# Expert weights of a mixture of experts: one plain unit of twelve in place of two, the token gate moved into the product of gate and up, a later release of the outcome buffers, and the weights of a further block requested together

## The chip, the cores and the metric

The kernel is one program on one NeuronCore of a Trainium2 chip, in one launch. The metric is the device time of that program in microseconds (us); less is better.

## The reference

Two blocks run one after the other over a sequence of 1024 tokens of width 1024, everything in float32. The first block is two layers of gated recurrences (they are not touched by the change). The second block is two layers, each an attention mixer, a layer norm with a scaled residual, and a mixture of experts of which each token uses two of 32:

```python
def hierarchical_moe(h, w_group, b_group, w_expert, b_expert, w_gate, w_up, w_down):
    ...
    gates = g_prob * e_prob
    experts = g_idx * EXPERTS_PER_GROUP + e_local
    ...
    def expert_block(args):
        xb, e = args
        return (jax.nn.silu(xb @ w_gate[e]) * (xb @ w_up[e])) @ w_down[e]

    ys = lax.map(expert_block, (xs, block_expert)).reshape(n_rows, D)
    ys = ys * row_gate[:, None].astype(ys.dtype)
    out = jnp.zeros((N + 1, D), ys.dtype).at[row_tok].add(ys)[:N]
    return out.reshape(B, S, D)
```

`xb` is 128 tokens by 1024, `w_gate` and `w_up` are 1024 by 512 per expert, `w_down` is 512 by 1024.

## The kernel before, in words

**What the expert stage does.** Per layer it walks over 32 experts of 128 places each. For one expert GpSimd (POOL) clears a buffer and gathers the expert's tokens into it (an indirect DMA, `slot<-xb`). TensorE (PE) transposes them: 8 transposes of 128x128 (`banks<-c,slot`, c being the unit matrix). ScalarE (ACT) and VectorE (DVE) turn the result into two rounded parts, high and low (`split`). Matmuls with gate and up follow, SiLU on ACT, the product `a` on DVE, 4 transposes of `a`, its split, and the matmuls with down. DVE multiplies the outcome by the token's gate and by a vector of the layer (`gn`) into a buffer `y`, and POOL scatters `y` with addition into the array Y in HBM (an indirect DMA, `Y<-slot`). The last expert keeps its outcome on the chip.

**Units.** The weights of one expert are 12 units of 128x1024 (512 KB): 4 of gate, 4 of up, 4 of down. A unit is used in one of two ways. A **split** unit is first rounded by ACT to a high part (`slot<-slot 128x1024` on ACT), then DVE subtracts to get the low part (`slot<-slot 128x1024` on DVE), and PE runs three products of these for each half, 6 matmuls of 512 columns. A **plain** unit is multiplied as it is, in full float32, against an unsplit copy of the transposed tokens (`xf`, in the tile named small): 2 matmuls in the program, 4 rows `banks<-slot,small` in the trace. `PLAIN` (L2479) names the plain units: unit 0 (the first of gate) and unit 4 (the first of up).

**What sets the order.** The program is written by cooperating chains of Python generators (`Flow`, L115). Each engine has a modelled clock, and the chain whose modelled time and priority come first records its next instructions; so the order on each engine follows from a model, and every engine then runs its list strictly in that order. Buffers are slots of 128x1024 in an arena (`Arena`, L281): `take` hands out the free slot with the smallest free time, and `give` notes as free time the modelled end of the last work on the slot (12 us after the issue for a scatter with addition). A slot that is taken again while its last work still runs on the chip makes the next writer wait.

**Chains of the stage.** `Experts.load` requests units in order on the queue of SyncE (SP), with at most `limit` units requested and not yet used up; `limit` is set to 20 while the output projection before the stage frees its slots (L1630), and to 22 when the stage starts (L2850). `Experts.split` splits at most `SPLIT = 6` units ahead of the one that PE has used last. `moe_experts` keeps up to two experts open, so that the transposes and the gate matmuls of the next expert stand among the down matmuls of the one before.

**The further block.** An expert with more than 128 tokens needs more blocks. `moe_extra` (L2712) holds a loop with a trip count that is known on the chip only, ahead of the 32 experts; its body is one `expert` whose weights come from `Direct` (L2693): 4 requests for gate at its first use, then for up and down, each at its own first use and behind the gather (`K.fetched`). In this input layer 0 makes no trip and layer 1 makes one.

**Rows ahead of the stage.** `Rows.put` (L1471) writes a finished tile of tokens: a modulated copy for the gather (`also`) and, after an affine step on POOL, the residual into Y.

All instructions of engines bear line L72 in the profile (a wrapper records them) and all DMAs of SP line L185.

## Time and profile before

| what | value |
|---|---|
| median of 3 runs | 4220.27 us |
| lowest and highest of them | 4214.49 and 4231.77 us |
| profiled execution, its own time | 4222.61 us |
| its span, first to last instruction | 4220.1 us |
| mean granted TensorE clock of the span | 0.957 |
| busy share of PE, DVE, ACT, POOL | 92%, 74%, 50%, 22% |
| expert stage of layer 0 in the trace | about 2035 to 2672 us |
| expert stage of layer 1 (with the further block) | about 3486 to 4170 us |

The profiled execution took 4222.61 us and its span is 4220.1 us, so 2.5 us lie around the span; it is 2.3 us above the median. Rows of the timeline give the start, the busy time, the engine, and in square brackets the idle time before the instruction with what ended it. The mean over the program hides the stages: with two expert stages of some 640 us each, rows by stretch tell more than the shares above.

### The profile page before, as it was taken

To read this page: it belongs to the slowest core of one execution; us is meant where nothing else is said; L and a number is where in the kernel's file an instruction comes from. 1 tells how busy PE (TensorE), PEld (TensorE's weight loads), DVE (VectorE), ACT (ScalarE), POOL (GpSimd) and SP (SyncE) were. 2 spreads that over 40 slices of the span, in tenths; PEclk is the share of its full clock that TensorE was granted. 3 is DMA by queue.
4 is the path that set the end of the run, shared out by engine and by line. 5 is a ranking of instruction groups with operands and counts; after the bars stand their busy time and mean duration, and the time that the engine had idled before them with its cause. 6 is when DMAs were issued, how large, how long until landed. Compare 5 with 4: busy or idle time off the path is not lost. (4 is left out here: it accounts for less than half of the span.)

```text
span 4220.1 us, 62468 instructions
## 1 busy us (share of the span) xinstructions
PE 3896.1 (92%) x22870; PEld 3126.8 (74%) x22870; DVE 3119.8 (74%) x5891; ACT 2118.6 (50%) x3866; POOL 946.2 (22%) x638
## 2 busy tenths in 40 slices
PE   7999999999999999969799999889999967999996
PEld 6888788788887777857577777677777765777774
DVE  7777766775767788686777777666667686777776
ACT  4333335342333555431466666667779415666663
POOL 2111100221113223354322222310001351222222
PEclk9999999999999999979899999999999978999998
DMA  4232322111113444234799998300011246999993
GB/s 150 80 98 84 95 90 92 42 42 51 53 61 120 146 131 135 68 122 153 269 356 357 355 355 314 117 11 21 16 53 41 96 161 226 353 351 357 360 353 128
DMA packets 338763, 682.11 MB, mean 162 GB/s; under 512 B 59957, under 2 KB 190703, under 8 KB 338453
## 3 DMA queue, kind: packets, MB, share of 16 engines
q1 hardware_dynamic: 320020, 644.95, 43.5%
q0 software_dynamic: 18432, 33.15, 3.2%
q8 instruction: 180, 2.95, 0.3%
q14 instruction: 131, 1.07, 0.1%
HBM read 625.89 MB, written 86.08 MB: 169 GB/s over the span
## 5 line engine op out<-in xcount | busy, mean ns | idle before, releaser
L72 PE MATMUL banks<-slot 128*128 128x512 f32 (+7 forms) x17868 | 3182.9, 344 | 78.7 <-DVE slot L72 44.1
L72 PEld LDWEIGHTS banks<-slot 128*128 128x128 f32 (+4 forms) x17868 | 2492.3, 178 | 643.6 <-issue 107.5
L72 DVE TENSOR_TENSOR slot<-slot 128x1024 fp32r<-128x1024 f32 (+14 forms) x1352 | 1308.2, 995 | 365.1 <-ACT slot L72 288.2
L72 ACT ACTIVATE slot<-slot 128x1024 fp32r<-128x1024 f32 (+5 forms) x946 | 927.0, 1009 | 876.6 <-PE banks L72 400.1
L72 ACT ACTIVATE slot<-banks 128x512 f32<-128x512 f32 (+8 forms) x1124 | 537.7, 497 | 677.0 <-PE banks L72 606.3
L72 POOL TENSOR_TENSOR slot<-slot 128x384 f32<-128x384 f32 (+3 forms) x270 | 452.7, 1696 | 1374.4 <-PE banks L72 402.0
L72 PE MATMUL banks<-c,slot 128*128 128x128 f32 (+2 forms) x3484 | 519.0, 285 | 118.3 <-DVE slot L72 53.9
L72 PEld LDWEIGHTS banks<-c,slot 128*128 128x128 f32 (+1 forms) x3484 | 430.8, 159 | 235.2 <-issue 66.6
L72 ACT ACTIVATE slot<-slot,small 128x1024 f32<-128x1024 f32 (+1 forms) x292 | 265.8, 924 | 197.3 <-DVE small L72 193.6
L72 PE MATMUL banks<-slot,small 128*128 128x512 f32 (+2 forms) x648 | 294.0, 573 | 49.1 <-ACT small L72 39.2
L72 DVE TENSOR_TENSOR slot<-banks,slot 64x512 fp32r<-64x512 f32 (+6 forms) x492 | 257.0, 551 | 62.5 <-ACT slot L72 52.5
L72 DVE COPY slot<-banks 128x512 f32<-128x512 f32 (+6 forms) x406 | 220.1, 551 | 103.7 <-PE banks L72 79.6
L72 POOL MEMSET slot<- 128x1024 f32 (+1 forms) x70 | 66.6, 957 | 940.3 <-PE banks L72 750.7
L72 PEld LDWEIGHTS banks<-slot,small 128*128 128x128 f32 x648 | 116.4, 213 | 105.3 <-ACT small L72 50.8
L72 POOL DMA_INDIRECT Y<-slot,small x62 | 144.0, 2322 | 198.5 <-DVE slot L72 183.5
L72 DVE TENSOR_REDUCE small<-banks 128x1 f32<-128x1024 f32 x128 | 154.4, 1220 | 45.7 <-PE banks L72 44.0
L72 ACT ACTIVATE slot<-banks,small 128x1024 f32<-128x1024 f32 x140 | 156.5, 1121 | 61.3 <-DVE small L72 60.5
L72 DVE TENSOR_TENSOR slot<-slot,banks 128x512 f32<-128x512 f32 (+3 forms) x175 | 116.5, 670 | 88.3 <-PE banks L72 88.0
L72 DVE SCALAR_TENSOR_TENSOR slot<-slot,c_act 128x1024 f32<-128x1024 f32 x84 | 121.0, 1442 | 29.4 <-DMA slot<-in_ada_w 22.7
L72 DVE SCALAR_TENSOR_TENSOR small<-small 128x1 f32<-128x1 f32 (+3 forms) x590 | 125.8, 220 | 12.6
L72 PE MATMUL banks<-small,slot 128*128 128x128 f32 (+1 forms) x576 | 105.4, 298 | 22.2 <-DVE small L72 18.4
L72 DVE SCALAR_TENSOR_TENSOR slot<-banks,cw,slot 128x511 f32<-128x511 f32 (+1 forms) x144 | 106.9, 746 | 6.0 <-ACT slot L72 3.9
(130 smaller groups left out, 1787.0 us busy)
## 6 DMA issues: line engine op xcount, KB each, us to landing
slot<-in_moe_w_up SPq DMA_DIRECT2D x260, 512.0 KB
slot<-in_moe_w_down SPq DMA_DIRECT2D x260, 512.0 KB
slot<-in_moe_w_gate SPq DMA_DIRECT2D x260, 512.0 KB
slot<-in_ada_w SPq DMA_DIRECT2D x96, 512.0 KB
slot<-in_w_in SPq DMA_DIRECT2D x56, 512.0 KB
xb<-slot SPq DMA_DIRECT2D x40, 512.0 KB
slot<-xb SPq DMA_DIRECT2D x24, 512.0 KB
slot<-in_na_w_qkv SPq DMA_DIRECT2D x24, 512.0 KB
```

The lines of the kernel that those rows point to most:

```text
L72: r = real(*a, **k)
```

## The change

It has six parts:

1. `PLAIN` becomes `(0,)`. Unit 4 is split like the others: 6 matmuls in place of 2 plain ones, one more rounding on ACT, one more subtraction on DVE, and the first half of the transposed tokens is split whole, not in its second 256 columns only.
2. The token gate moves: `a` becomes (SiLU times gate) times up in one DVE instruction, and `y` is a product of two.
3. `y` goes back to the arena when the scatter's modelled end has passed on the recording clock (`stored`), not at once; in the further block it goes back at once as before.
4. `Direct` requests all 12 units at the start of the loop's body, and splits the gate units right after the gather's issue (`first`).
5. The `limit` ahead of the stage is 16, not 20.
6. For the last two tiles of tokens `Rows.put` records the affine step and the write of Y only after the routing (`mid.late`).

```diff
+        if self.late is not None and t >= NT - 2:
+            yield self.late
         with K.F.aside():
             if self.early:
                 self.affine(K, x)
...
-        freed.limit = 20
+        freed.limit = 16
...
-PLAIN = (0, 4)
+PLAIN = (0,)
...
         if not g:
             F.scalar.activation(xf.f[:, 0:2 * c], p.f[:, 0:2 * c], AF.Copy)
-        o, m = (0, 4 * c) if g else (2 * c, 2 * c)
-        split(K, xh.r[:, 4 * g * c + o:4 * g * c + o + m], xl.r[:, 4 * g * c + o:4 * g * c + o + m], p.f[:, o:o + m])
+        split(K, xh.r[:, 4 * g * c:4 * g * c + 4 * c], xl.r[:, 4 * g * c:4 * g * c + 4 * c], p.f[:, :4 * c])
...
-    V.tensor_mul(a.f[:c, 0:512], a.f[:c, 0:512], ps[1].f[:c])
+    V.scalar_tensor_tensor(a.f[:c, 0:512], a.f[:c, 0:512], gate[:c], ps[1].f[:c], op0=ALU.mult, op1=ALU.mult)
...
-        V.scalar_tensor_tensor(y.f[:c, s], ps[n].f[:c], gate[:c], gn.f[:c, s], op0=ALU.mult, op1=ALU.mult)
+        V.tensor_mul(y.f[:c, s], ps[n].f[:c], gn.f[:c, s])
...
+    def stored():
+
+        yield from F.until(F.last(y.f))
+        A.give(y)
+
     with F.aside():
         F.gpsimd.indirect_dma_start(out=Y, ...
-    A.give(y)
+    if later:
+        F.spawn(stored(), 0)
+    else:
+        A.give(y)
...
+    def ask(self, i):
+        K = self.K
+        w = units_of(K.I[EXPERT_W[i]][self.l][bass.ds(self.e, 1)], i)
+        self.b.append((yield from several(K.A, 4)))
+        for m in range(4):
+            K.F.dma(self.b[i][m].f, w[:, m])
+
+    def first(self):
+
+        for n in range(4):
+            b = self.b[0][n]
+            self.w.append((b,) if n in PLAIN else (yield from self.halves(b)))
...
         e = nc.values_load(num[0:1, 1:2], engines=[mybir.EngineType.SP], min_val=0, max_val=31)
+        w = Direct(K, l, e)
+        for i in range(3):
+            for _ in w.ask(i):
+                pass
...
+    mid.late = M.routed
```

Where the scheduler puts the work now, at three places. In these rows a name such as slot_18021 is one use of a slot; the high part of a split has the number n and the low part n+1.

First place, PE, at the change from one expert to the next in the middle of layer 0. Before (slot_17558 holds the gathered tokens of the next expert, slot_18079 the product `a`, slot_17897 the plain first unit of gate, slot_18141 the split transposed `a`, slot_18043 a unit of down):

```order
8351 L72 MATMUL banks_67<-c32_68,slot_17558 128x128 [waits DMASW7_49]
8352 L72 MATMUL banks_67<-c32_68,slot_17558 128x128 x7
8353 L72 MATMUL banks_67<-slot_17897,small_66 128x512 [waits DMAHW7_49,Activation_49]
8354 L72 MATMUL banks_67<-c32_68,slot_18079 128x128 [waits DVE_49]
8355 L72 MATMUL banks_67<-c32_68,slot_18079 128x128 x3
8356 L72 MATMUL banks_67<-slot_17897,small_66 128x512
8357 L72 MATMUL banks_67<-slot_18043,slot_18141 128x512 [waits Activation_49]
8358 L72 MATMUL banks_67<-slot_18044,slot_18141 128x512
```

The same place now (slot_17454 holds the tokens, slot_17975 is `a`, slot_17781 the plain unit, slot_18026 and slot_18027 the high and low part of the tokens, slot_18021 and slot_18041 the second and third unit of gate, slot_17955 the first of down, slot_18049 the split `a`):

```order
8324 L72 MATMUL banks_67<-c32_68,slot_17454 128x128 [waits DMASW5_49]
8325 L72 MATMUL banks_67<-c32_68,slot_17454 128x128 x7
8326 L72 MATMUL banks_67<-c32_68,slot_17975 128x128 [waits DVE_49]
8327 L72 MATMUL banks_67<-c32_68,slot_17975 128x128 x3
8328 L72 MATMUL banks_67<-slot_17781,small_66 128x512 [waits DMAHW3_49,Activation_49]
8329 L72 MATMUL banks_67<-slot_17781,small_66 128x512
8330 L72 MATMUL banks_67<-slot_18021,slot_18026 128x512 [waits Activation_49]
8331 L72 MATMUL banks_67<-slot_18022,slot_18026 128x512
8332 L72 MATMUL banks_67<-slot_18021,slot_18027 128x512 [waits DVE_49]
...
8336 L72 MATMUL banks_67<-slot_18041,slot_18026 128x512 [waits Activation_49]
...
8342 L72 MATMUL banks_67<-slot_17955,slot_18049 128x512 [waits Activation_49]
```

The transposes of `a` moved up behind those of the tokens, ahead of both halves of the plain unit, and two units of gate now stand between the plain unit and the first matmul of down.

Second place, DVE, at the same change of expert. Before (slot_18158 the low part of a weight unit, slot_18079 `a`, slot_18123 the low part of the tokens, slot_18141 the low part of the transposed `a`):

```order
3294 L72 TENSOR_TENSOR slot_18158<-slot_17927,slot_18157 128x1024 [waits DMAHW2_49,PE_49,Activation_49]
3295 L72 TENSOR_TENSOR slot_18079<-slot_18079,banks_67 128x512 [waits PE_49]
3296 L72 TENSOR_TENSOR slot_18170<-slot_17951,slot_18169 128x1024 [waits DMAHW4_49,Activation_49]
3297 L72 TENSOR_TENSOR slot_18123<-banks_67,slot_18122 128x256 [waits PE_49,Activation_49]
3298 L72 TENSOR_TENSOR slot_18123<-banks_67,slot_18122 128x512 [waits Activation_49]
3299 L72 TENSOR_TENSOR slot_18141<-banks_67,slot_18141 128x512 [waits Activation_49]
```

The same place now (slot_18022, slot_18042 and slot_18066 low parts of weight units, slot_17975 `a`):

```order
3290 L72 TENSOR_TENSOR slot_18022<-slot_17793,slot_18021 128x1024 [waits DMAHW4_49,PE_49,Activation_49]
3291 L72 TENSOR_TENSOR slot_18042<-slot_17811,slot_18041 128x1024 [waits DMAHW5_49,DVE_49,Activation_49]
3292 L72 SCALAR_TENSOR_TENSOR slot_17975<-slot_17975,small_66,banks_67 128x512 [waits PE_49]
3293 L72 TENSOR_TENSOR slot_18066<-slot_17823,slot_18065 128x1024 [waits DMAHW6_49,Activation_49]
3294 L72 TENSOR_TENSOR slot_18027<-banks_67,slot_18026 128x512 [waits PE_49,Activation_49]
3295 L72 TENSOR_TENSOR slot_18027<-banks_67,slot_18026 128x512 [waits Activation_49]
3296 L72 TENSOR_TENSOR slot_18049<-banks_67,slot_18049 128x512 [waits Activation_49]
```

The order of kinds is the same, but the subtraction just ahead of `a` belongs to the unit whose rounding waits for the second unit of up; before it waited for the third, by the values of PE's semaphore that these rows wait for.

Third place, ACT, at the third expert from the end of layer 0. Before (slot_21513 is the SiLU of that expert, the others are roundings; the semaphores DMASW are those of gathers and scatters, and DMASW6 in row 1909 is that of the scatter issued just before):

```order
1906 L72 ACTIVATE slot_21539<-slot_21348 128x1024 [waits DMAHW4_49,PE_49]
1907 L72 ACTIVATE slot_21551<-slot_21358 128x1024 [waits DMAHW5_49,PE_49]
1908 L72 ACTIVATE slot_21513<-banks_67 128x512 [waits DMASW0_49,PE_49]
1909 L72 ACTIVATE slot_21641<-slot_21442 128x1024 [waits DMAHW3_49,DMASW6_49,DVE_49]
1910 L72 ACTIVATE slot_21591<-slot_21366 128x1024 [waits DMAHW6_49,DVE_49]
```

The same place now (slot_21582 is the SiLU):

```order
1917 L72 ACTIVATE slot_21582<-banks_67 128x512 [waits PE_49]
1918 L72 ACTIVATE slot_21567<-slot_21343 128x1024 [waits DMAHW3_49]
1919 L72 ACTIVATE slot_21592<-slot_21355 128x1024 [waits DMAHW4_49,DVE_49]
1920 L72 ACTIVATE slot_21604<-slot_21367 128x1024 [waits DMAHW5_49,DVE_49]
1921 L72 ACTIVATE slot_21616<-slot_21379 128x1024 [waits DMAHW6_49]
1922 L72 ACTIVATE small_66<-banks_67 128x256 [waits PE_49]
1923 L72 ACTIVATE slot_21633<-banks_67 128x512
```

No rounding behind the SiLU waits for a scatter there any more.

## Rows read from the trace of the kernel before

**Rows 1.** Busy us of PE, PEld, DVE, ACT, POOL; clock, DMA share, GB/s; layer 0's experts.

```profile
2300.00:2400.00 100.00, 97.64 (x417) 73.47 (x416) 79.18 (x84) 63.73 (x78) 26.47 (x17) 1.00 0.99 360
```

**Rows 2.** Groups of instructions by shape, 2100 to 2600 us: busy, mean ns, idle before.

```profile
L72 DVE TENSOR_TENSOR slot<-slot 128x1024 fp32r<-128x1024 f32 x259 | 305.3, 1220 | 101.1 <-ACT slot L72 101.1
L72 ACT ACTIVATE slot<-slot 128x1024 fp32r<-128x1024 f32 x259 | 263.0, 1054 | 161.9 <-PE banks L72 146.1 <-DVE slot L72 13.8
L72 PE MATMUL banks<-slot,small 128*128 128x512 f32 x208 | 104.8, 605 | 12.3 <-ACT small L72 12.3
```

**Rows 3.** Timeline of PE over one expert in layer 0.

```profile
2401.89 1.88 PE L72 MATMUL banks<-slot,small 128*128 128x512 f32 x4
...
2407.71 1.11 PE L72 MATMUL banks<-c,slot 128*128 128x128 f32 x8
2409.29 1.12 PE L72 MATMUL banks<-slot,small 128*128 128x512 f32 x2 [0.47 <-ACT small L72]
2410.25 0.60 PE L72 MATMUL banks<-c,slot 128*128 128x128 f32 x4
2410.69 1.02 PE L72 MATMUL banks<-slot,small 128*128 128x512 f32 x2
2411.54 9.83 PE L72 MATMUL banks<-slot 128*128 128x512 f32 x42
2421.20 1.02 PE L72 MATMUL banks<-slot,small 128*128 128x512 f32 x2
```

**Rows 4.** Timeline of ACT: roundings released by one PE unit after another.

```profile
2607.62 1.06 ACT L72 ACTIVATE slot<-slot 128x1024 fp32r<-128x1024 f32 x1 [0.29 <-PE banks L72]
2608.98 1.06 ACT L72 ACTIVATE slot<-slot 128x1024 fp32r<-128x1024 f32 x1 [0.30 <-PE banks L72]
```

**Rows 5.** Timeline of DVE at the change of expert of rows 3.

```profile
2407.73 1.22 DVE L72 TENSOR_TENSOR slot<-slot 128x1024 fp32r<-128x1024 f32 x1 [3.07 <-ACT slot L72]
2408.87 0.68 DVE L72 TENSOR_TENSOR slot<-slot,banks 128x512 f32<-128x512 f32 x1
```

**Rows 6.** Timeline near the end of layer 0: a scatter, ACT, PE.

```profile
2611.53 2.28 POOL L72 DMA_INDIRECT Y<-slot,small  x1 [13.78 <-DVE slot L72]
...
2621.70 2.95 ACT L72 ACTIVATE slot<-slot 128x1024 fp32r<-128x1024 f32 x3 [6.20 <-issue]
...
2625.62 1.12 PE L72 MATMUL banks<-c,slot 128*128 128x128 f32 x4 [4.69 <-DVE slot L72]
```

**Rows 7.** Timeline after the first scatter of layer 0: ACT, then PE.

```profile
2076.25 2.95 ACT L72 ACTIVATE slot<-slot 128x1024 fp32r<-128x1024 f32 x3 [7.20 <-DMA Y<-slot,small]
...
2079.52 1.22 PE L72 MATMUL banks<-slot,small 128*128 128x512 f32 x1 [6.52 <-ACT small L72]
```

**Rows 8.** Timeline of PE at the same two places of layer 1.

```profile
3574.97 2.07 PE L72 MATMUL banks<-slot,small 128*128 128x512 f32 x2 [6.26 <-ACT small L72]
...
4122.70 1.11 PE L72 MATMUL banks<-c,slot 128*128 128x128 f32 x4 [4.87 <-DVE slot L72]
```

**Rows 9.** DMA queues, 2100 to 2600 us: packets, MB, share of 16 engines.

```profile
q1 hardware_dynamic: 45010, 163.88, 87.2%
q0 software_dynamic: 7290, 13.28, 10.7%
```

**Rows 10.** Timeline of SP: the last requests for weights of layer 0.

```profile
2618.64 12.04 SPq L185 DMA_DIRECT2D slot<-in_moe_w_down  x4
```

**Rows 11.** The further block in layer 1: gather, then PE.

```profile
3497.41 1.28 POOL L72 DMA_INDIRECT slot<-xb,slot  x1 [9.95 <-DMA slot<-in_moe_w_gate]
...
3500.93 1.98 PE L72 MATMUL banks<-c,slot 128*128 128x128 f32 x8 [5.56 <-DMA slot<-xb,slot]
...
3518.54 2.17 PE L72 MATMUL banks<-slot 128*128 128x512 f32 x5 [0.94 <-ACT slot L72]
```

**Rows 12.** DMA issues, 2100 to 2600 us: median us from issue to landing.

```profile
Y<-slot,small POOLq DMA_INDIRECT x26, 10.5
slot<-xb,small POOLq DMA_INDIRECT x25, 7.2
```

More of the change, by code (lines that the diff above doesn't have):

```diff
@@ L1477, in __init__ @@
         self.x, self.g, self.b, self.early, self.also, self.mod = x, g, b, early, also, mod
-        self.rows = []
+        self.rows, self.late = [], None
     def prepare(self, K, user, write=False):
@@ L2551, in done, with expert @@
             self.ahead -= 1
-def expert(K, get, tok, gate, gn, rows, Y, x=None, hold=None):
+def expert(K, get, tok, gate, gn, rows, Y, x=None, hold=None, later=True):
     F, T, V, A = K.F, K.F.tensor, K.F.vector, K.A
@@ L2560, in expert @@
         x = yield from gather(K, tok, rows)
+        yield from get.first()
     yield
@@ L2695, in __init__ @@
         self.K, self.l, self.e = K, l, e
-    def next(self, i, n):
-        K = self.K
-        if n == 0:
-            w = units_of(K.I[EXPERT_W[i]][self.l][bass.ds(self.e, 1)], i)
-            self.b = yield from several(K.A, 4)
-            for m in range(4):
-                K.F.dma(self.b[m].f, w[:, m], K.fetched if i else None)
-        if 4 * i + n in PLAIN:
-            return (self.b[n],)
-        return (yield from self.halves(self.b[n]))
+        self.b, self.w = [], []
+    def ask(self, i):
[8 more added lines that the diff above has]
+            self.w.append((b,) if n in PLAIN else (yield from self.halves(b)))
+    def next(self, i, n):
+        if i == 0:
+            return self.w[n]
+        b = self.b[i][n]
+        return (b,) if 4 * i + n in PLAIN else (yield from self.halves(b))
     def done(self, bufs):
@@ L2761, in moe_extra @@
         block()
-        for _ in expert(K, Direct(K, l, e), tok, gate[:, 2:3], gn, rows, Y):
+        for _ in expert(K, w, tok, gate[:, 2:3], gn, rows, Y, later=False):
             pass
```

## The prediction

> **What bounds the kernel now.** I read the views from coarse to fine. The busy times by stretch come first: inside an expert stage PE is busy for 97.6 of 100 us at full clock, DVE for 79.2 and ACT for 63.7, and the DMA engines are busy for 99% of the time [rows 1]. So PE paces the stage, with the DMA engines close behind. The timeline of PE then gives one expert: the plain unit of up starts at 2401.89 and the next expert's at 2421.20, a period of 19.31 us [rows 3]. Within it PE waits once for another engine: 0.47 us for ACT's copy of the tokens (`xf`) after the 8 transposes [rows 3]; the groups say the same for all 26 experts of the stretch, 12.3 us [rows 2]. Last come the places where the period breaks. Near both ends of both expert stages ACT takes a slot whose scatter has not landed: 10.2 us after the scatter's issue it goes on (2611.53 to 2621.70), and PE has lost 4.69 us [rows 6]; in layer 1 it is 4.87 us [rows 8]. At the first scatter of a layer ACT waits 7.20 us, and PE loses 6.52 and 6.26 us [rows 7, 8].
>
> **Part 1, the plain unit.** A plain unit costs PE 1.70 us: half of one runs from 2410.69 to 2411.54 [rows 3]. A split unit costs 1.36 us: that is the distance at which PE releases one rounding of ACT after the other [rows 4]. The change replaces one by the other in 32 experts of layer 0 and 33 of layer 1 (the further block included): 65 x 0.34 = 22 us less on PE. ACT gets one rounding more, 1.05 us, and DVE one subtraction more, 1.22 us [rows 2]. Both lie beside PE as long as the engines have room: ACT goes from 12.3 to 13.4 us per expert, about 72%; DVE from 15.3 us per expert (79.2% of 19.31) to 16.5, and with the longer split of the tokens (between 0 and another half us) to about 16.8 of a period of some 18.5. If that cover goes, rival 3 is what it costs.
>
> The rows put six matmuls of 512 columns at 1.36 us, 0.227 us each [rows 4]. The Trainium skill (TensorE: Matmul & The Clock Gate, Step-by-step: what each phase is for) gives a distance of about 216 ns for such a matmul. By that page a split unit would cost 1.30 us and this term would be 26 us; the row decides, and I keep 22.
>
> **The change of expert.** This follows from the order, not from the diff. Let T be the end of the last matmul of up, 2407.71 [rows 3]. Before: 8 transposes until T+1.11, then the wait until `xf` is there at T+1.58, half of the plain unit, 4 transposes of `a` (0.44 us), the other half, and the next units from T+3.83. Now the transposes of `a` stand ahead of the plain unit. They fill T+1.11 to T+1.55, so that `xf` is missed for 0.03 us in place of 0.47. The condition is that `a` is ready by T+1.11. Before it was ready only at T+1.84 (2408.87 plus 0.68), as DVE did a subtraction first that ended then [rows 5] and whose rounding waits for the third unit of up. Now that place belongs to a rounding which waits for the second unit, 1.36 us earlier; so `a` is bound by T itself plus its own 0.7 us, about T+0.9. With some 30 undisturbed changes per layer: 60 x 0.44 = 26 us less. Two more gains I leave to the range: the plain unit is no longer cut in two (its first half took 0.96 us with the change of operand, not 0.85: 0.11 us per expert), and the low part of the transposed `a` now has two gate units as cover (the 42 matmuls before took 9.66 us where 0.227 each make 9.53: 0.13 us) [rows 3]: at most 14 us together.
>
> **Part 2, the token gate.** One DVE instruction gets an operand and two lose one; all keep their size. The nearest rows differ by less than 0.1 us for an instruction of 512 columns, so I take nothing for it, within +/-0.1 us per expert, hidden as above.
>
> **Part 3, the outcome buffers.** At the end of a layer the rounding behind the SiLU no longer waits for a scatter. The next writer of such a slot stands 13 DVE instructions of 1.1 to 1.2 us later, near 15 us, against a landing of 10.5 us [rows 12]. So the stalls of 4.69 and 4.87 us go: 9.6 us [rows 6, 8]. What the clock loses after them (0 to 3 us each) stays in the range. At the first scatter of a layer the wait remains, as the order still has a rounding in front of the `xf` copy that takes the first `y` slot: only two roundings, not three, now stand between the landing and the copy, so PE's loss falls by one, 1.0 us per layer: 2 us [rows 7]. Bounds are nothing and the whole 12.8 us.
>
> **Part 4, the further block.** It runs once. Before, the units of up and down were asked for late; what PE visibly waited for ACT ahead of down is 0.94 us [rows 11]. Against it stands the gather, 3.5 us from issue to first transpose (3497.41 to 3500.93) [rows 11], which now shares the engines with 8 more units: in the full stage a gather takes 7.2 us [rows 12]. Bounds: 2 us less to 3.7 us more. I take nothing, as both are small and of opposite sign.
>
> **Parts 5 and 6.** Four units less are there when the stage starts, 4 x 1.40 us of DMA time (below). With 16 units of 1.4 to 1.7 us in hand, over 20 us, the next request lands long before its use, so I take nothing; bounds 0 to 5.6 us per layer. The delayed writes of Y hardly move in the order; nothing.
>
> **The sum.** 22 + 26 + 9.6 + 2 = 60 us. The profiled execution took 4222.6 us (span 4220.1 and 2.5 around it), 2.3 us above the median of the runs. 4222.6 - 60 = 4162.6, and against the median **4160 us**. A measurement of this kernel can tell 0.5%, 21 us, from no change.
>
> **Rival 1: `a` comes late.** If DVE runs behind by one subtraction, `a` is ready at T+1.84 as now, its transposes (some 0.1 us behind it) end at T+2.4 and the plain unit at T+4.1, 0.27 us later than now. Of the 0.34 us of the unit 0.07 stay: 60 x 0.07 + 11.6 = 16 us, **4204 us**. For it: DVE at 91%. Against it: before each `y` DVE has to wait for PE, which lets it catch up every period.
>
> **Rival 2: the DMA engines bind.** The 26 experts of the stretch took 87.2% of 500 us for their weights and 10.7% for gathers and scatters [rows 9]: 16.8 us, 1.40 per unit, and 2.06, together 18.8 us per expert. PE would want 18.53. If nothing buffers it, 60 x 0.3 = 18 us are lost: **4178 us**. Against it: the requests run ahead; the last one of layer 0 leaves by 2630.7 [rows 10], some 40 us ahead of the end of the stage, more than the 9 us that a layer would fall behind.
>
> A harder form: the transfers already have all the bandwidth they can get, 360 GB/s [rows 1], the period stays 19.31, and only the stalls go, 12 us: **4208 us**. The Trainium skill (DMA: Bandwidth & Descriptors, Specifications) gives about 358 GB/s as one core's limit at HBM; by that rule the row is at its end already. The lead speaks against this form too.
>
> **Rival 3: DVE binds, slower than before.** DVE waits 101.1 us for ACT in 26 experts, 3.9 us each [rows 2]. If these waits stay whole beside 16.8 us of work, the period is 20.7 us, 1.4 more: 60 x 1.4 - 12 = 72 us, **4292 us**. It turns slower from 2.5 us of waits that stay. Against it: ACT in turn waits for PE (146.1 of its 161.9 us [rows 2]), so these waits shrink when DVE is late.
>
> **Rival 4: the later release does nothing on the chip.** It orders by modelled clocks only; if the chip is off by a few us, the stalls at the ends remain: **4170 us**.
>
> **How the numbers follow.** The forecast has 0.55, rival 1 0.15, rival 2 0.14 and 0.05 for its harder form, rival 3 0.06, rival 4 0.05. The low end takes the forecast with the gains left out (14 of the change of expert, 6 of the clock, 2 of the block, 3 of the first scatter): 4135. The high end is rival 1, 4204. Beyond lie the harder form, rival 3 and some of the tails, below 0.2. Faster by over 0.5% (below 4199): forecast, rivals 2 and 4, and a third of rival 1, which may come in part: 0.79. Within 0.5%: the rest of rival 1 and the harder form: 0.15. Slower: 0.06.
>
> **What would show it.** In the timeline of PE: 12 transposes in a row, a period of 18.3 to 18.7 us, and no wait over 0.1 us for `xf`; a wait of the transposes of `a` for DVE of near 0.9 us would be rival 1. In the waits: PE or ACT waiting for weights in flight would be rival 2. In the busy times: DVE over 95% with PE below 95%, rival 3. At the ends of the stages PE's idle times of 4.7 and 4.9 us should be gone, and those of 6 us at the first scatters be some 5.5. The forecast is wrong if the period in the stage is above 18.8 us.

## The result and the profile after

The changed kernel takes 4152.2 us (median of 4 runs, 4146.9 to 4164.4) against 4223.5 us of the kernel before on the same chip: ratio 0.9832, 95% interval 0.9812 to 0.9851. The forecast was 4160 us, with 4135 to 4204 as its range. The profiled execution took 4151.2 us and its span is 4149.4 us, 70.7 us below the span before; the mean granted clock is 0.957 in both.

Busy times by stretch, in the columns of [rows 1]:

```profile
2300.00:2400.00 100.00, 99.54 (x446) 79.16 (x445) 88.67 (x92) 71.22 (x84) 25.44 (x17) 1.00 0.99 367
```

PE went from 97.64 to 99.54 of 100 us, DVE from 79 to 89, ACT from 64 to 71. The groups by shape, 2100 to 2600 us, answer to [rows 2]:

```profile
L72 DVE TENSOR_TENSOR slot<-slot 128x1024 fp32r<-128x1024 f32 x299 | 352.2, 1219 | 3.8 <-ACT slot L72 0.4 <-PE banks L72 0.3
...
L72 ACT ACTIVATE slot<-slot 128x1024 fp32r<-128x1024 f32 x299 | 306.5, 1065 | 68.7 <-PE banks L72 64.2 <-DMA slot<-in_moe_w_up 1.7 <-DMA slot<-in_moe_w_down 1.4
...
L72 PE MATMUL banks<-slot,small 128*128 128x512 f32 x108 | 52.3, 599 | 0.5 <-ACT small L72 0.5
```

PE's 12.3 us of waits for `xf` became 0.5, and the 101.1 us that DVE spent waiting for ACT in front of its subtractions became 3.8. The timeline of PE over one expert shows the new order:

```profile
2405.44 1.66 PE L72 MATMUL banks<-c,slot 128*128 128x128 f32 x12
2406.93 1.88 PE L72 MATMUL banks<-slot,small 128*128 128x512 f32 x4
2408.25 15.58 PE L72 MATMUL banks<-slot 128*128 128x512 f32 x66
2423.68 1.66 PE L72 MATMUL banks<-c,slot 128*128 128x128 f32 x12
2425.17 1.88 PE L72 MATMUL banks<-slot,small 128*128 128x512 f32 x4
```

From one plain unit to the next are 18.24 us, where [rows 3] had 19.31. Twelve transposes stand in a row and nothing waits. A few changes of expert per layer keep an older form and take 18.4 to 18.6 us, so the mean over layer 1 (24 copies of `xf` on ACT) is 18.29. The timeline of DVE at 2405.44, the end of the last matmul of up, has `a` as its next instruction, with no subtraction ahead of it as in [rows 5]:

```profile
2405.64 0.75 DVE L72 SCALAR_TENSOR_TENSOR slot<-slot,small,banks 128x512 f32<-128x512 f32 x1 [1.51 <-PE banks L72]
```

**Where the period breaks.** The idle times of 4.69 and 4.87 us near the ends of the layers [rows 6, 8] are gone. Those at the first scatters [rows 7, 8] went from 6.5 and 6.3 to 4.1 us, in layer 0 and layer 1. In layer 0 ACT still takes a slot whose scatter has not landed, with the later release in place (timelines of ACT and PE):

```profile
2072.58 2.00 ACT L72 ACTIVATE slot<-slot 128x1024 fp32r<-128x1024 f32 x2 [5.30 <-DMA Y<-slot,small]
...
2074.90 3.78 PE L72 MATMUL banks<-slot,small 128*128 128x512 f32 x4 [4.12 <-ACT small L72]
...
3541.60 3.46 PE L72 MATMUL banks<-slot,small 128*128 128x512 f32 x4 [4.14 <-ACT small L72]
```

A wait is new, at the end of layer 0. The last scatter leaves, SP reads Y back, and PE stands for it with the last matmuls of down queued behind (timeline of POOL, SP and PE):

```profile
2620.09 2.28 POOL L72 DMA_INDIRECT Y<-slot,small  x1 [15.95 <-DVE slot L72]
...
2626.88 3.93 SPq L185 DMA_DIRECT2D slot<-Y  x8
...
2630.48 2.08 PE L72 MATMUL banks<-slot,c 128*128 128x512 f32 x2 [4.16 <-DMA slot<-Y]
2631.57 8.47 PE L72 MATMUL banks<-slot 128*128 128x512 f32 x24
```

From the scatter to the matmul are 10.4 us. Before, the same chain took 9.8 us, but PE reached that place only 1.0 us ahead of it:

```profile
2654.74 1.55 POOL L72 DMA_INDIRECT Y<-slot,small  x1 [16.51 <-DVE slot L72]
...
2664.56 1.13 PE L72 MATMUL banks<-slot,c 128*128 128x512 f32 x2 [1.00 <-DMA slot<-Y]
...
2666.81 5.77 PE L72 MATMUL banks<-slot 128*128 128x512 f32 x24
```

And the 24 matmuls behind the wait now take 8.47 us, 0.35 each, where they took 5.77 before. Behind the 4.16 us of idle time the granted TensorE clock is 0.50, the lower of its two levels (1.2 of 2.4 GHz), for 5 us; in the kernel before it is 1.00 over the same 24 matmuls. Busy times by stretch, in the columns of [rows 1]:

```profile
2630.48:2635.50 5.02, 5.02 (x10) 3.32 (x11) 0.00 (x0) 0.00 (x0) 0.00 (x0) 0.50 1.03 416
```

**The ledger.** Setting the two timelines side by side at places that both have: the stretch from the start of the layer-0 stage to its last transposes of `a` is 38.6 us shorter, the tail behind it 7.3 us longer (4.2 of it is the wait for Y, 2.7 the 24 matmuls at the lower clock); the further block is 1.4 us longer; the layer-1 stage is 39.8 us shorter, its tail 1.0 us longer; 1.2 us come ahead of the stages and some 0.7 between them. That makes 70.6 us. So the gain lies where it was expected, inside the two stages, at 1.07 us per undisturbed expert.

The DMA queues, 2100 to 2600 us, moved more than before [rows 9] in the same time. First the total before, then the changed kernel:

```profile
DMA packets 52334, 177.57 MB, mean 355 GB/s; under 512 B 9059, under 2 KB 9059, under 8 KB 52300
```

```profile
DMA packets 54370, 184.50 MB, mean 369 GB/s; under 512 B 9408, under 2 KB 9408, under 8 KB 54334
...
q1 hardware_dynamic: 46846, 170.58, 88.0%
q0 software_dynamic: 7488, 13.48, 10.9%
```

### The profile page after: what moved, and what is told of

Its sections match the earlier page's. It is cut to its first block, busy times and chain, and to the rows that moved or that the text cites. A ratio compares the mean times of both kernels' runs of the same rounds, so it can differ in the third digit from the quotient of the medians.

```text
span 4149.4 us, 62801 instructions
## 1 busy us (share of the span) xinstructions
PE 3854.3 (93%) x23000; PEld 3149.1 (76%) x23000; DVE 3207.2 (77%) x5956; ACT 2194.5 (53%) x3931; POOL 919.6 (22%) x638
## 5 line engine op out<-in xcount | busy, mean ns | idle before, releaser
L72 PE MATMUL banks<-slot 128*128 128x512 f32 (+8 forms) x18258 | 3249.2, 345 | 81.5 <-DVE slot L72 45.5
L72 PEld LDWEIGHTS banks<-slot 128*128 128x128 f32 (+5 forms) x18258 | 2565.3, 178 | 624.9 <-issue 93.1
L72 DVE TENSOR_TENSOR slot<-slot 128x1024 fp32r<-128x1024 f32 (+14 forms) x1417 | 1378.0, 1001 | 129.1 <-ACT slot L72 65.5
L72 ACT ACTIVATE slot<-slot 128x1024 fp32r<-128x1024 f32 (+5 forms) x1011 | 996.5, 1019 | 663.4 <-PE banks L72 233.3
L72 ACT ACTIVATE slot<-banks 128x512 f32<-128x512 f32 (+8 forms) x1124 | 548.7, 510 | 678.0 <-PE banks L72 611.5
L72 PE MATMUL banks<-c,slot 128*128 128x128 f32 (+2 forms) x3484 | 514.5, 285 | 110.8 <-DVE slot L72 41.8
L72 DVE TENSOR_TENSOR slot<-banks,slot 128x512 fp32r<-128x512 f32 (+4 forms) x622 | 364.9, 608 | 164.2 <-PE banks L72 92.0
L72 PE MATMUL banks<-slot,small 128*128 128x512 f32 (+2 forms) x388 | 158.0, 544 | 19.5 <-ACT small L72 10.2
L72 ACT ACTIVATE small<-banks 128x64 f32<-128x64 f32 (+2 forms) x289 | 78.0, 274 | 96.9 <-PE banks L72 90.7
L72 DVE TENSOR_TENSOR slot<-slot,banks 128x512 f32<-128x512 f32 (+4 forms) x110 | 72.2, 664 | 69.9 <-PE banks L72 69.0
L72 PEld LDWEIGHTS banks<-small,slot 128*128 128x128 f32 (+1 forms) x576 | 83.6, 200 | 40.4 <-DVE small L72 16.8
```

The lines of the kernel that those rows point to most:

```text
L72: r = real(*a, **k)
```

## The experiments

The kernel before was run beside each set, so kernels are compared by their ratio to it. The intervals reach some 0.002 to 0.003 to each side, about 10 us; the period of an expert, which repeats within 0.02 us, is the sharper measure. "Old order" below is 8 transposes, half a plain unit, 4 transposes; "new order" is 12 transposes in a row.

### Everything but the unit

```diff
-PLAIN = (0,)
+PLAIN = (0, 4)
```

> The changed kernel with units 0 and 4 plain again (token gate, release, further block and the limit of 16 as changed); PE's order at the change of expert is that of before (8 transposes, half a plain unit, 4 transposes, the other half). Theory: the plain unit and the order that comes with it carry the gain, so the period is 19.2 to 19.4 us again with a wait of 0.47 us for xf in each, and the time 4205 to 4222 us. Rival (release, prefetch limit or token gate carry it): the period stays below 18.6 and the time below 4175 us.

Measured: 4199.9 us, ratio 0.9934 (0.9909 to 0.9958), 5 us under the expected range. The order is the old one and PE waits for `xf` again. The timeline of PE:

```profile
2399.78 1.88 PE L72 MATMUL banks<-slot,small 128*128 128x512 f32 x4
...
2407.18 1.13 PE L72 MATMUL banks<-slot,small 128*128 128x512 f32 x2 [0.47 <-ACT small L72]
...
2408.57 1.02 PE L72 MATMUL banks<-slot,small 128*128 128x512 f32 x2
2409.03 10.13 PE L72 MATMUL banks<-slot 128*128 128x512 f32 x42
2419.00 1.88 PE L72 MATMUL banks<-slot,small 128*128 128x512 f32 x4
```

The period is 19.22 us. The other parts alone are worth some 28 us. Most of it is the idle times at the first scatters and at the ends, none of which is left here (22.3 us in [rows 6 to 8]); the rest is the period, 0.09 us shorter in the same order of transposes. Nearly all of that lies behind the second half of the plain unit of gate: from there to the plain unit of up are 10.43 us, and 10.51 before (2410.69 to 2421.20, [rows 3]). Before, the next matmul is the first of down; it needs ACT's rounding of the transposed `a`, which ends at 2411.49, and starts at 2411.54. Here a unit of gate stands there and starts at 2409.03, while that rounding goes on until 2409.53 (timelines of ACT, before and then here):

```profile
2410.89 0.60 ACT L72 ACTIVATE slot<-banks 128x512 fp32r<-128x512 f32 x1 [0.89 <-PE banks L72]
```

```profile
2408.92 0.61 ACT L72 ACTIVATE slot<-banks 128x512 fp32r<-128x512 f32 x1
```

### The unit and nothing else

```diff
-PLAIN = (0, 4)
+PLAIN = (0,)
...
-        o, m = (0, 4 * c) if g else (2 * c, 2 * c)
-        split(K, xh.r[:, 4 * g * c + o:4 * g * c + o + m], xl.r[:, 4 * g * c + o:4 * g * c + o + m], p.f[:, o:o + m])
+        split(K, xh.r[:, 4 * g * c:4 * g * c + 4 * c], xl.r[:, 4 * g * c:4 * g * c + 4 * c], p.f[:, :4 * c])
```

(on the kernel before)

> The kernel before with unit 4 split and nothing else changed (limit 20, token gate with y, old further block); PE's order at the change of expert is that of the changed kernel (12 transposes in a row, then the plain unit). Theory: nearly the whole gain, period 18.2 to 18.4 us, time 4148 to 4165 us. Rival: the time stays above 4190 us as the other parts are missing.

Measured: 4147.3 us, ratio 0.9808 (0.9784 to 0.9832). One constant and one line give all of the gain, as far as the intervals can tell. The timeline of PE:

```profile
2396.69 1.60 PE L72 MATMUL banks<-c,slot 128*128 128x128 f32 x12
2398.12 1.89 PE L72 MATMUL banks<-slot,small 128*128 128x512 f32 x4
2399.45 15.58 PE L72 MATMUL banks<-slot 128*128 128x512 f32 x66
2414.87 1.60 PE L72 MATMUL banks<-c,slot 128*128 128x128 f32 x12
```

The new order comes without any of the other parts, and the period is 18.18 us, 0.06 less than in the changed kernel. The idle times at the ends are gone too, with `y` given back at once.

### The limit ahead of the stage

```diff
-        freed.limit = 16
+        freed.limit = 20
```

(on the changed kernel)

> The changed kernel with the limit ahead of the stage at 20 again, which moves nothing but the order: PE's order at the change of expert falls back to 8 transposes, half the plain unit, 4 transposes, the other half, with one plain unit of twelve. So it tells the unit from the order. Theory (the unit is worth 0.35 to 0.4 us and the order the rest): period 18.8 to 19.0 us with the wait of 0.47 us for xf, time 4185 to 4200 us. Rival A (the unit carries all): period 18.2 to 18.4 us, time 4145 to 4160 us.

Measured: 4177.6 us, ratio 0.9886 (0.9862 to 0.991), 7 us under the expected range. The timeline of PE has the old order and its wait:

```profile
2405.90 1.11 PE L72 MATMUL banks<-c,slot 128*128 128x128 f32 x8
2407.48 1.12 PE L72 MATMUL banks<-slot,small 128*128 128x512 f32 x2 [0.47 <-ACT small L72]
...
2424.72 1.11 PE L72 MATMUL banks<-c,slot 128*128 128x128 f32 x8
```

The period is 18.82 us. So 16 in place of 20 is worth 0.58 us per expert here, in the middle of a stage in which the limit is 22 in both. The number shifts the modelled clocks, and the generators of the stage fall into another order. What four units less ahead of the stage cost by themselves, this run can't separate. The kernel with the unit alone has the new order at limit 20.

### The new order without the unit

```diff
-            self._flow.spend(self._name, self._cost(op, a, k), outs, ins, (12.0 if "compute_op" in k else 3.0) if "dma" in op else 0.0)
+            self._flow.spend(self._name, self._cost(op, a, k), outs, ins, (18.0 if "compute_op" in k else 3.0) if "dma" in op else 0.0)
```

(on the kernel before: the modelled length of a scatter, which no instruction contains)

> The kernel before with one number changed: the model reckons a scatter with addition at 18 us in place of 12. Both units stay plain; what moves is the order. In the program 45 of some 60 changes of expert now have the 12 transposes in a row (none but 4 before), and the copy that waited for the first scatter of a layer no longer does. My theory (the order of the change of expert is a gain of its own, 0.44 us as predicted to 0.58 us as the run with limit 20 gives it, with or without the unit): 45 x 0.44 to 0.58 = 20 to 26 us, and the first-scatter stalls of 6.5 and 6.3 us gone: 4185 to 4192, with a period of 18.75 to 18.9 us where the 12 transposes stand. Rival (the transposes of a are ready early only because unit 4 is split, so the order without the unit gains nothing): only stalls go, 4210 to 4215, and PE waits some 0.7 us for DVE behind the eighth transpose.

Measured: 4177.1 us, ratio 0.9906 (0.9883 to 0.9929). The timelines of PE and DVE:

```profile
2393.80 1.60 PE L72 MATMUL banks<-c,slot 128*128 128x128 f32 x12
2395.24 1.89 PE L72 MATMUL banks<-slot,small 128*128 128x512 f32 x4
2396.56 10.15 PE L72 MATMUL banks<-slot 128*128 128x512 f32 x42
2406.56 1.88 PE L72 MATMUL banks<-slot,small 128*128 128x512 f32 x4
...
2412.38 1.60 PE L72 MATMUL banks<-c,slot 128*128 128x128 f32 x12
```

```profile
2394.00 0.69 DVE L72 TENSOR_TENSOR slot<-slot,banks 128x512 f32<-128x512 f32 x1 [1.88 <-PE banks L72]
```

My theory holds and was too small. The period is 18.57 us: 0.74 less than before, by order alone, with both units plain. `a` starts 0.20 us after the last matmul of up, so the split unit is not what lets `a` be early. The part on the first scatters was wrong: PE still loses 6.65 us (2069.67) and 5.56 us (3546.85) there, and a new idle time of 2.70 us for `xf` stands at 2132.41. The time came out lower all the same: 45 x 0.74 = 33 us and the stalls at the ends, which are gone here too, 9.6 us, make 43 us, less the new 2.7, for 41.8 measured on that chip.

### The same model for the changed kernel

The same one number on the changed kernel, in two sessions; in the second the changed kernel itself ran beside it.

> The changed kernel with the same one number: a scatter is reckoned at 18 us. 48 changes of expert have the 12 transposes in a row (42 in the changed kernel), and no copy of xf waits for the first scatter. If the idle times that are left at the first scatters (4.12 and 4.14 us) are lost time, they come out whole, with 6 x 0.58 = 3.5 us from the order: 4151 - 8.3 - 3.5 = 4139 to 4143. Rival (the DMA engines are at their end in the stage, 99% busy, so that what PE doesn't wait for here it waits for at the stage's end): 4148 to 4152, and new waits for weights in flight.

> The changed kernel with the scatter reckoned at 18 us, once more, beside the changed kernel itself on the same chip. Its first look lost none of the 4 us at the first scatters. If that is worth its 8.3 us and the two new changes of expert 3.5 us, the ratio to the kernel before is 0.0028 below that of the changed kernel: 0.980 against 0.983. Rival (the difference came from the runs' spread): the two ratios agree within 0.001.

> The changed kernel itself, on the chip of the run beside it: ratio 0.983, 0.981 to 0.985 as first measured.

Measured: 4139.1 us, ratio 0.9805 (0.9784 to 0.9826), and again 4139.7 us, 0.9796 (0.9778 to 0.9814); the changed kernel again 4150.5 us, 0.9831 (0.9811 to 0.985). No idle time above 1 us is left at the first scatters. The rival with the DMA engines at their end falls: the gain stays. In the tail of layer 0 the wait for Y is gone and a later one for ACT is longer in its place (4.65 us at 2643.39, 1.74 in the changed kernel).

### The same model with the unit alone

> The kernel before with one plain unit (as in the run of the unit alone, 4147) and the scatter reckoned at 18 us; none of the change's other parts. 36 changes of expert have the 12 transposes in a row, 47 in the run of the unit alone: 11 x 0.58 = 6.4 us more; the first-scatter idle times of 3.9 and 5.0 us go, 8.9 us less. Theory: 4142 to 4147, the two effects near cancelling. Rival (the order of the change of expert makes no difference once unit 4 is split): 4136 to 4139.

Measured: 4156.5 us, ratio 0.985 (0.9834 to 0.9867): slower than the unit alone, and neither theory. The stalls at the first scatters did not go: they stand in front of the transposes of `a` now, 5.78 us at 2084.68 and 5.72 us at 3546.82. And 11 changes of expert have the old order with its wait of 0.47 us for `xf` and take 18.83 us. At one more, PE waits for DVE. The timelines of DVE and PE there:

```profile
2394.78 1.23 DVE L72 TENSOR_TENSOR slot<-slot 128x1024 fp32r<-128x1024 f32 x1 [1.02 <-ACT slot L72]
2395.93 0.68 DVE L72 TENSOR_TENSOR slot<-slot,banks 128x512 f32<-128x512 f32 x1
```

```profile
2395.09 1.11 PE L72 MATMUL banks<-c,slot 128*128 128x128 f32 x8
2396.66 0.66 PE L72 MATMUL banks<-c,slot 128*128 128x128 f32 x4 [0.46 <-DVE slot L72]
```

This is rival 1 of the prediction at work, at this one change of expert: a subtraction stands ahead of `a`, and PE waits 0.46 us. It is a matter of the recorded order, and in the stretches of the changed kernel shown above it does not happen.

### No plain unit

```diff
-PLAIN = (0,)
+PLAIN = ()
```

(on the changed kernel)

> The changed kernel with no plain unit: all 12 are split (the copy xf is still made, and unused). It asks what binds next. If PE still sets the pace, it gains another unit, 65 x 0.34 to 0.49 = 22 to 32 us: 4120 to 4130, period 17.75 to 17.9 us. If the DMA engines bind (88.0% and 10.9% of 500 us for 27.4 experts are 18.05 us each), the period stops at 18.05 us: 4138 to 4142, with PE below 99% and waiting for weights. If DVE binds (448 of 500 us in the changed kernel, 16.35 us per expert and 1.22 more), 17.6 us if it never waits, 19.2 us if its 1.6 us of waits stay: 4150 to 4210, DVE above 95% and PE waiting for it.

Measured: 4161.4 us, ratio 0.9864 (0.9841 to 0.9887): no gain. Busy times by stretch, then the timelines of DVE and PE at a change of expert:

```profile
2100.00:2600.00 500.00, 488.02 (x2268) 402.12 (x2267) 472.05 (x486) 381.69 (x458) 128.09 (x75) 1.00 0.99 366
```

```profile
2418.01 0.74 DVE L72 SCALAR_TENSOR_TENSOR slot<-slot,small,banks 128x512 f32<-128x512 f32 x1
...
2418.81 1.13 PE L72 MATMUL banks<-c,slot 128*128 128x128 f32 x8 [0.87 <-DVE slot L72]
```

DVE is busy 94.4% and PE 97.6%, and PE waits for `a`. PE's waits in these 500 us are 8.7 us for DVE and 2.5 us for ACT, some 0.4 us per expert, as much as the unit was to gain; the mean period is 18.56 us. So DVE is what PE meets next, in the direction of the third theory, though DVE stays under the 95% that the theory asked for. Whether DVE is too slow, or only asked too early, is open: the order is again another one (in the rows above 8 transposes stand behind the wait), and no run has this kernel in the order of 12 in a row. The DMA engines moved 366 GB/s, no more than in the changed kernel.

### The token gate back in the outcome

```diff
-    V.scalar_tensor_tensor(a.f[:c, 0:512], a.f[:c, 0:512], gate[:c], ps[1].f[:c], op0=ALU.mult, op1=ALU.mult)
+    V.tensor_mul(a.f[:c, 0:512], a.f[:c, 0:512], ps[1].f[:c])
...
-        V.tensor_mul(y.f[:c, s], ps[n].f[:c], gn.f[:c, s])
+        V.scalar_tensor_tensor(y.f[:c, s], ps[n].f[:c], gate[:c], gn.f[:c, s], op0=ALU.mult, op1=ALU.mult)
```

(on the changed kernel)

> The changed kernel with the token gate back in the outcome: a is a product of two again, y a product of three. The order of the change of expert stays the new one. DVE gets one operand more in two instructions and loses it in one. Theory (the gate's place is worth nothing, DVE has room): 4150 to 4154 by the measure of the changed kernel, ratio 0.982 to 0.985, period 18.2 to 18.3 us. Rival (the place of the gate is what lets DVE be in time for a, or its width counts): period above 18.4 us and 4165 or more.

Measured: 4140.7 us, ratio 0.9806 (0.9784 to 0.9827), better than both theories. The product `a` in the groups by shape, first in the changed kernel, then here:

```profile
L72 DVE SCALAR_TENSOR_TENSOR slot<-slot,small,banks 128x512 f32<-128x512 f32 x27 | 20.2, 748 | 14.7 <-PE banks L72 14.7
```

```profile
L72 DVE TENSOR_TENSOR slot<-slot,banks 128x512 f32<-128x512 f32 x28 | 19.3, 688 | 14.8 <-PE banks L72 14.8
```

The wide form takes 0.06 us longer, and since `a` is now the last thing that the 12 transposes need, PE pays it: the row of 12 takes 1.66 us in the changed kernel and 1.60 here, the period 18.24 and 18.18. Over the 42 changes of expert that have the 12 transposes in a row this is 2.5 us (those of the older form take 18.38 to 18.60 us in both); the stalls at the first scatters are 2.90 and 2.92 us here (2 x 1.2 less). Together they are 5 us of the 10 by which this run lies below the changed kernel beside it (4150.5 us); the rest is within the intervals.

### Both

The changed kernel with the scatter at 18 us and the gate back in the outcome.

> The changed kernel with both edits that made it faster: the scatter reckoned at 18 us and the token gate back in the outcome. 46 changes of expert have the 12 transposes in a row; no copy waits for the first scatter. If the two gains add (the wider product of gate and up holds PE up for 0.06 us per expert, 18.18 in place of 18.24 us: 60 x 0.06 = 3.6 us; the first scatters 2 x 4.1 us): ratio 0.979, 4135 to 4138. Rival (only the first scatters count in both, and e9's gain was 2 x 1.2 us of these and spread): 0.980 as the run with 18 us alone, 4140, period 18.24 us.

Measured: 4136.6 us, ratio 0.9794 (0.9766 to 0.9823). The lowest median of all, with a period of 18.18 us; but from the run with 18 us alone (0.9796) the time can't tell it. An idle time of 2.70 us for `xf` is new, at 3555.78, early in layer 1.

### The further block's requests behind the gather

```diff
-            K.F.dma(self.b[i][m].f, w[:, m])
+            K.F.dma(self.b[i][m].f, w[:, m], K.fetched if i else None)
...
     def first(self):
+        for i in (1, 2):
+            yield from self.ask(i)
...
-        for i in range(3):
-            for _ in w.ask(i):
-                pass
+        for _ in w.ask(0):
+            pass
```

(on the changed kernel)

> The changed kernel, whose further block requests up and down (8 units together) only when the gather has landed, gate first as now. Theory (the 8 units slow the gather): gather to first transpose 3.5 us in place of 7.4, and the block's end to end, from the gather's issue to the scatter's, 28 to 30 us in place of 31.2. Rival (the gather is slow for another reason): the gather takes 7 us as now. In the whole time 2 us, too little to see.

Measured, in a single run: 4157.1 us, from which nothing follows. The gather on POOL and the first transpose on PE, in the changed kernel and then here:

```profile
3464.13 1.29 POOL L72 DMA_INDIRECT slot<-xb,slot  x1 [9.94 <-DMA slot<-in_moe_w_gate]
...
3471.51 1.98 PE L72 MATMUL banks<-c,slot 128*128 128x128 f32 x8 [9.41 <-DMA slot<-xb,slot]
```

```profile
3471.36 1.28 POOL L72 DMA_INDIRECT slot<-xb,slot  x1 [9.94 <-DMA slot<-in_moe_w_gate]
...
3474.84 1.98 PE L72 MATMUL banks<-c,slot 128*128 128x128 f32 x8 [5.52 <-DMA slot<-xb,slot]
```

From the gather to the transposes are 7.4 us with the 8 units of up and down in flight, and 3.5 us without. Where the units are asked for behind the gather, 1.5 us of the block come back (54.95 against 56.45 us from the block's first token counts on PE to the first transposes of the stage). From the gather's issue to the scatter's are 29.8 us, as expected, for 31.2 in the changed kernel. In the whole time that can't be seen.

## Why the prediction was right

The time, 4152 us, lies 8 us under the forecast, and the signs that it named are there: a period below 18.8 us, 12 transposes in a row, no wait for `xf`, the idle times at the ends gone. Its two main terms are the two causes, both sized too low, and one term was credited to the wrong part. That the number came so close owes something to luck: the two terms measured 61 us in place of 48, and the tails and the further block, which the sum had at nothing, took 9.7 back.

The periods of seven kernels take the gain apart:

| plain units | order | token gate in | kernel | period, us |
|---|---|---|---|---|
| 2 | old | `y` | before | 19.31 |
| 2 | old | `a` | all but the unit | 19.22 |
| 2 | new | `y` | before, scatter 18 us | 18.57 |
| 1 | old | `a` | after, limit 20 | 18.82 |
| 1 | new | `a` | after | 18.24 |
| 1 | new | `y` | unit alone; after with gate in `y` | 18.18 |

**The plain unit: 0.39 to 0.40 us, not 0.34.** 18.57 to 18.18 in the new order, 19.22 to 18.82 in the old; 65 times that is 26 us, for the 22 of the prediction. The split unit was right: ACT's roundings still follow one another at 1.36 us.

```profile
2378.85 1.06 ACT L72 ACTIVATE slot<-slot 128x1024 fp32r<-128x1024 f32 x1 [1.43 <-PE banks L72]
2380.21 1.06 ACT L72 ACTIVATE slot<-slot 128x1024 fp32r<-128x1024 f32 x1 [0.30 <-PE banks L72]
```

What was too small is the plain one, taken as twice the 0.85 us between the starts of two groups. The same rows have it: from the plain unit of up (2401.89) to the end of the last matmul of up (2407.71) are 5.82 us, and three split units of 1.36 leave 1.74 of them [rows 3]; that less 1.36 is 0.38. In the new order, with 11 split units (14.96 us) and the 1.43 us from the first of the 12 transposes to the plain unit, 1.79 us are left of 18.18 for it. The Trainium skill's 216 ns per matmul (TensorE: Matmul & The Clock Gate, Step-by-step: what each phase is for), which the prediction weighed, would have given 26 us as well, but by a split unit of 1.30 us, which these rows don't show.

**The change of expert: 0.74 us with two plain units, 0.58 with one, not 0.44.** The two differ by more than the units: the first pair of rows has the gate in `y`, the second has it in `a` and starts from the old order that is 0.09 us shorter. The 0.74 comes in two pieces. The first is the transposes. Before, 8 transposes and the wait behind them took 1.58 us and 4 more transposes 0.44 [rows 3]; in the run of the new order without the unit all 12 take 1.44 us to the plain unit (2393.80 to 2395.24), 0.58 less. The prediction had 1.55 and 0.03 of waiting for them, and so 0.44. The second is what it left to the range, 0.11 for the plain unit cut in two and 0.13 for the low part of the transposed `a`: the plain unit and the 42 matmuls behind it took 0.96, 0.85 and 9.66 us [rows 3] and now take 11.32 (2395.24 to 2406.56), 0.15 less, of the 0.24. That belongs in the sum: it was worked out from rows and had no reason against it. The condition that it named is the right one (`a` starts 0.20 us after the last matmul of up), but its reason was not: it put this down to the rounding that unit 4 frees earlier, and the kernel before does the same with both units plain once the order is the new one.

**Part 2, the gate: 0.06 us per expert in the new order, not nothing.** The size was read rightly (under 0.1 us), the cover wrongly. The same reordering that the prediction counted on puts `a` on PE's path, and with it every ns of its width.

**Part 3, the outcome buffers: nothing.** Without `stored`, with `y` given back at once, the changed program is the same list of instructions with the same waits on every engine; so it was not run. The same holds in the old order: the release alone leaves the kernel before as it is, and without it the kernels with two plain units and with the limit at 20 stay as they are. The step that credited the 9.6 us to the later release failed. The stalls at the ends are gone in the unit alone and in the kernel before with the scatter at 18 us, neither of which has the release. Another order takes other slots; which of them mattered was not traced. Rival 4 was right that the release does nothing, and wrong that the stalls then stay. At the first scatters the loss fell by 2.4 and 2.1 us, where the prediction had 1 each; how much is lost there (0 to 6.7 us over the runs) depends on the order too.

**Part 4: 1.4 us more,** inside the bounds of 2 less to 3.7 more. The gather does slow down, to 7.4 us, as the row of the full stage said; most of that comes back later in the block.

**Part 5: nothing as argued, some 23 us in fact** (ratio 0.9832 against 0.9886). The argument was about four units less in flight, and what these cost no run separates. But the number enters the model, and with 20 in its place the changed kernel has the old order. The prediction read the order itself, so its sum was not hurt; its price for this part was.

**Part 6** was taken as nothing; without it the changes of expert stand as they do, and it was not run.

**Missed: the tail of layer 0,** some 7 us. PE reaches the last transposes earlier, the scatter and its reading back take their 10 us as before, and PE waits 4.16 us; then it runs at the lower clock, which costs another 2.7 us. The prediction reckoned with such a loss of the clock, but for the stalls that went, not for one that came.

**The sum again,** by what was measured: over 60 changes 1.02 us (mean period 19.31 to 18.29) make 61; the ends 9.6 and the first scatters 4.5; less 7.3, 1.0 and 1.4: 65 of 70.7 us. The rest was not traced.

**The rivals.** Rival 1 is real but did not come here (the run with the unit and 18 us shows it at one change of expert). Rival 3 may start one unit further on: without a plain unit PE waits for DVE, though in another order. Rival 2 fell in both forms. The harder one would have kept the period at 19.31 us with the transfers at 360 GB/s; in the same 100 us they took 367 GB/s, and over 500 us 369 where it was 355. The Trainium skill's 358 GB/s for one core (DMA: Bandwidth & Descriptors, Specifications), which that row gets as half of a stack's 716 GB/s for two cores, is thus not the end for this program on its one core: the trace of after disagrees. Which bandwidth would be the end stays open, as in no run PE waited for weights between 2100 and 2600 us: in the changed kernel ACT's roundings waited 3.1 us for them.

**Left open.** Which modelled clock decides between the two orders (a limit of 16 or 20, a scatter of 12 or 18 us and one plain unit or two each tip it, in no direction that I could foretell).

## What to carry to other kernels

Where a model of time writes the order, an edit of the work and an edit of the order come together: run the edit alone and the order alone before crediting either. Here a single number of the model that no instruction contains gave some 40 us, 9.6 of them stalls, more than the 26 us of the unit itself, and three of the change's six parts (the gate, the release and the further block) gave nothing or cost a little. When a reordering puts an instruction on the path of the busiest engine, price that instruction anew: its width was free before. And a gain that is worked out from rows and has nothing against it belongs in the sum, not in the range.

## What the runs showed that I had not expected

- DMA engines that are 98 to 99% busy in the profile are not at their end: the same engines moved 355 GB/s before and 369 GB/s after, over 500 us, with slices of up to 415 GB/s.
- A gather into a buffer of 128 rows takes 3.5 us to its first use with few transfers in flight and 7.4 us with 8 units of 512 KB more.
- A DVE product of three operands with 512 columns takes 748 ns, of two 688 ns.
